# Three loads of x on ScalarE's queue, and the first block of x transposed into a bank of its own

## The chip, the cores and the metric

The kernel runs on one core of one Trainium2 chip. The metric is the device time of one execution in microseconds (us); lower is better. TensorE (PE) multiplies matrices, VectorE (DVE), ScalarE (ACT) and GpSimd (POOL) work element by element, and SyncE (SP) issues transfers between device memory and the core's own memory. A profile shows one execution; times in it count from the start of its span.

## The reference

One decoder block on 256 tokens of width 1024, all in float32. Cut to what matters here:

```python
u = rmsnorm(h, norm_mix_pre[l])          # h is x at first: 256 x 1024
z = u @ w_in[l]                          # 1024 x 4096
p = z[..., :o_q]
q = z[..., o_q:o_k].reshape(B, S, N_HEADS, HEAD_DIM)
k = z[..., o_k:o_v].reshape(B, S, N_HEADS, HEAD_DIM)
v = z[..., o_v:o_g].reshape(B, S, N_HEADS, HEAD_DIM)
g = z[..., o_g:] + b_gate[l]
...                                      # pooling and attention, gated, w_out, residual
u2 = rmsnorm(h, norm_mlp_pre[l])
a = jnp.square(jax.nn.relu(u2 @ w_up[l]))
h = h + rmsnorm(a @ w_down[l], norm_mlp_post[l])
```

The change touches only the start: the loads of x, its transposition, and the products for `v`.

## The kernel before

The 256 tokens are two tiles (t = 0, 1) of 128; the width 1024 is eight blocks (k = 0 to 7) of 128. Every matrix product is made of three: an operand is split into a high part (`_h`, rounded to the multiplier's format) and a low part (`_l`, the rest), and `mm3` adds high by high, high by low and low by high into one accumulator bank. A weight block is loaded raw (`_r`), ACT writes the high part, and DVE (11 of 16 columns) and POOL (the other 5) write the low part (`share_lo`). The order of the work is the order in which the code is written: each engine takes its instructions one by one as they stand, and waits where an operand isn't there.

The kernel starts with the products for `v`. The names:

- `x_sb[t, n]` is one of four pieces of x, 128 tokens by 512 columns (256 KB): n = 0 holds blocks 0 to 3, n = 1 blocks 4 to 7. `load_x(t, n)` issues its load.
- `v_r` with k = 0 to 7 are eight weight pieces, 128 by 512 (256 KB), loaded one by one by `load_v(k)`.
- `turn_x(t, n)` transposes the four blocks of a piece on PE into one bank `x_ps{t}{n}`, which `u_parts(k, t)` reads: ACT scales a block by the gain and writes its high part `uh`, then DVE its low part `ul`. The row factor of the norm is applied later.
- `v_rows(t, k)` is one `mm3` into bank `v_ps{t}`: three products with 512 columns.
- `split_v(k)` makes the high and low part of a weight piece. For k = 0 the high part is made by DVE (a cast), not by ACT.
- `keep_busy(n)` puts n small products of constants on PE.

Eight accumulator banks are in use in turn. All loads at the start are issued by SP, in the order x(0,0), the gain, v0, v1, x(1,0), v2, x(0,1), v3, x(1,1), v4 to v7, then the blocks for q. On PE stand the transposes of x(0,0), nine fillers, the products (t=0, k=0), the transposes of x(1,0), the products (0,1) and (1,0), the transposes of x(0,1), the products (1,1), and so on for k = 2 to 7. After `v` come q, k, p and the gates, pooling and attention, the output projection and the MLP (`up`, `dn`), with weights streamed through three raw buffers.

Of the kernel before, what the change touches and what calls it, by code (L numbers as in the profile page):

```python
# [16 lines left out]
P = 128  # L17
# [3 lines left out]
KD = D // P  # L21
# [12 lines left out]
def hybrid_block(ctx: ExitStack, tc: tile.TileContext, x, norm_mix_pre, w_in, b_gate, pool_w, pool_scale,  # L34
# [4 lines left out]
    nc = tc.nc  # L39
# [10 lines left out]
    def bank(name):  # L50
        return psum.tile([P, 512], F32, tag="bank", name=name)
# [7 lines left out]
    def keep_busy(n):  # L59
        for _ in range(n):  # L60
            nc.tensor.matmul(busy[:, 0:P], fill, fill, start=True, stop=True)
# [6 lines left out]
    ident = const.tile([P, P], F32, name="ident")  # L68
# [81 lines left out]
    def load_next():  # L150
        if done[0] < len(order):
            order[done[0]].load_all()
            done[0] += 1
# [12 lines left out]

    x_sb = act.tile([P, NT, D], F32, name="x_sb")

    def load_x(t, n):
        c = slice(n * 512, (n + 1) * 512)  # L170
        nc.sync.dma_start(x_sb[:, t, c], x[0, t * P:(t + 1) * P, c])


    class Columns:
# [12 lines left out]
        def turn(self):  # L187
            ps = bank(self.name + "_ps")
            nc.tensor.transpose(ps[:, 0:self.n], self.row, ident[0:self.n, 0:self.n])
            nc.vector.tensor_copy(self.col, ps[:, 0:self.n])  # L190
# [4 lines left out]
    g_mix = Columns("g_mix", [(norm_mix_pre, KD)], "oTh")  # L195
# [3 lines left out]
    def load_v(k):  # L199
        bv[k // 4].load(k % 4)  # L200

    load_x(0, 0)
    g_mix.load()
    load_v(0)
    load_v(1)
    load_x(1, 0)
    load_v(2)
    load_x(0, 1)
    load_v(3)
    load_x(1, 1)  # L210
    for k in range(4, KD):
        load_v(k)
    load_next()
    others.load()

# [12 lines left out]
    def mm3(ps, whl, rhl, start, stop, last=0):  # L228

        (wh, wl), (rh, rl) = whl, rhl  # L230
        second, third = ((wh, rl), (wl, rh)) if last == 0 else ((wl, rh), (wh, rl))
        nc.tensor.matmul(ps, wh, rh, start=start, stop=False, skip_group_check=True)  # L232
        nc.tensor.matmul(ps, *second, start=False, stop=False, skip_group_check=True)  # L233
        nc.tensor.matmul(ps, *third, start=False, stop=stop, skip_group_check=True)  # L234
# [23 lines left out]
    def tokens(hl, k, t):  # L258
        c = slice(t * P, (t + 1) * P)
        return hl[0][:, k, c], hl[1][:, k, c]  # L260
# [5 lines left out]
    def narrow(blocks, k, c=slice(0, 512)):  # L266
        b = blocks[k // 4]
        return b.hi[:, k % 4, c], b.lo[:, k % 4, c]

    def placed(pool, blocks, tag, name, at, room=128):  # L270


        t = pool.tile([P, blocks * S + room], F32R, tag=tag, name=name)
        return t[:, at:at + blocks * S].rearrange("p (k s) -> p k s", k=blocks)
# [50 lines left out]
    def scaled_parts(hl, k, t, ps, gain):  # L325
        c = slice(t * P, (t + 1) * P)
        v = ps[:, (k % 4) * P:(k % 4 + 1) * P]
        hi, lo = hl[0][:, k, c], hl[1][:, k, c]
        nc.scalar.activation(hi, v, AF.Copy, scale=gain)
        nc.vector.scalar_tensor_tensor(lo, v, gain, hi.bitcast(F32), op0=ALU.mult, op1=ALU.subtract)  # L330
# [14 lines left out]
    u = tuple(placed(act, KD, f"uT_{i}", f"u{i}", 112) for i in "hl")  # L345
# [6 lines left out]
        yield from rstd(ss, rr[t])  # L352

    def u_parts(k, t):
        scaled_parts(u, k, t, xT[t, k // 4], g_mix[k])

    vps = [bank(f"v_ps{t}") for t in range(NT)]

    def v_rows(t, k, last=0):
        mm3(vps[t], tokens(u, k, t), narrow(bv, k), k == 0, k == KD - 1, last)  # L360
# [3 lines left out]
    xT = {}  # L364

    def turn_x(t, n):
        xT[t, n] = turn(x_sb[:, t, :], n, f"x_ps{t}{n}")

    def split_v(k):
        bv[k // 4].split_piece(k % 4, True)  # L370

    g_mix.turn()
    turn_x(0, 0)
    keep_busy(9)
    nc.vector.tensor_copy(bv[0].hi[:, 0, :], bv[0].raw[:, 0, :])
    u_parts(0, 0)
    bv[0].share_lo(0)
    v_rows(0, 0, last=1)
    u_parts(1, 0)
    turn_x(1, 0)  # L380
    split_v(1)
    v_rows(0, 1)
    u_parts(0, 1)
    v_rows(1, 0)
    turn_x(0, 1)
# [590 lines left out]
```

## Time and profile before

| | us |
|---|---|
| median of 3 runs | 340.37 (340.05 to 341.89) |
| the profiled execution | 339.66 |
| its span (first to last instruction) | 337.9 |
| PE busy | 329.9 (98%) |
| PE's weight loads busy | 305.0 (90%) |
| DVE, ACT, POOL busy | 220.3, 182.2, 77.9 |
| read from device memory | 61.10 MB, 184 GB/s over the span |

Busy time of PE is modelled and overlaps with its weight loads, so 98% says that PE is nearly always in use, not that it runs at its peak. The chain of waits follows the work that ended last back to the start, and names at each step what released it. In lists of waits each row has the time in total, the number of waits and the longest; in timelines each row has the start, the length, the engine, the line, the operation and, in brackets, how long the engine was idle before it and what ended that. SPq and ACTq are the queues in which an engine's transfers are issued; an issue is short, and the transfer lands later.

### The profile page before, as it was taken

How to read it: one execution, taken by the hardware profiler on the slowest of the kernel's cores; microseconds unless marked ns; L12 is line 12 of the kernel's file. 1: busy time of each engine (PE TensorE's matmuls, PEld its weight loads, DVE VectorE, ACT ScalarE, POOL GpSimd, SP SyncE). 2: the span in 40 equal slices, each digit the busy share in tenths (PEclk: the TensorE clock that was granted, in tenths of full speed). 3: DMA queues.
4: the chain of work that ended last, by engine and by line, in shares of the span. 5: the costliest groups of instructions: out<-in, count | busy, mean ns of one | idle time of the engine just before them, and what ended most of it. 6: DMA issues, size and time to landing. Idle time of an engine off the chain costs nothing.

```text
span 337.9 us, 5701 instructions
## 1 busy us (share of the span) xinstructions
PE 329.9 (98%) x2325; PEld 305.0 (90%) x2325; DVE 220.3 (65%) x292; ACT 182.2 (54%) x256; POOL 77.9 (23%) x68
## 2 busy tenths in 40 slices
PE   8999999999999999999999999999999999999992
PEld 7799999999999999888898998989989989899881
DVE  3899777998385789376686746637366374653535
ACT  3984678665837755175768436354263551544331
POOL 3698589155305000056600000000000000000000
PEclk9999999999999999999999999999999999999999
DMA  6996971644555946707355854907629267090003
GB/s 211 375 324 216 222 232 27 237 151 140 209 189 207 353 135 240 248 4 248 124 176 198 288 211 139 330 30 263 236 74 317 109 236 262 11 353 14 0 0 124
DMA packets 27363, 63.04 MB, mean 187 GB/s; under 512 B 1317, under 2 KB 2761, under 8 KB 27337
## 3 DMA queue, kind: packets, MB, share of 16 engines
q1 hardware_dynamic: 26760, 62.15, 53.4%
q0 software_dynamic: 576, 0.52, 1.2%
q8 instruction: 18, 0.29, 0.4%
q14 instruction: 9, 0.07, 0.1%
HBM read 61.10 MB, written 1.05 MB: 184 GB/s over the span
## 4 chain that ended last, share of the span: by engine, by line
PE 96%; DMA 1%; DVE 1%; SPq 0%; DVEq 0%; ACT 0%; issue 0%; ACTq 0%
PE up_ps L232 9%; PE up_ps L234 9%; PE up_ps L233 9%; PE d_ps L242 7%; PE d_ps L241 7%; PE d_ps L245 7%; PE g_ps L232 4%; PE g_ps L233 4%; PE g_ps L234 4%; PE wo_ps L241 2%; PE wo_ps L242 2%; PE wo_ps L245 2%; DMA x_sb<-in_x_dram 1%; PE q_ps L232 1%; PE p_ps L234 1%; PE q_ps L234 1%
## 5 line engine op out<-in xcount | busy, mean ns | idle before, releaser
L232 PE MATMUL up_ps<-u2h,up_h 128*128 128x256 f32 x224 | 62.1, 277 | 0.0
L233 PE MATMUL up_ps<-u2l,up_h 128*128 128x256 f32 x224 | 61.9, 276 | 0.0
L234 PE MATMUL up_ps<-u2h,up_l 128*128 128x256 f32 x224 | 61.9, 276 | 0.0
L93 DVE TENSOR_TENSOR dn_l<-dn_r,dn_h 128x2048 fp32r<-128x2048 f32 x16 | 36.5, 2292 | 16.4 <-ACT dn_h L89 16.3
L233 PEld LDWEIGHTS up_ps<-u2l,up_h 128*128 128x128 f32 x224 | 42.1, 188 | 0.0
L232 PEld LDWEIGHTS up_ps<-u2h,up_h 128*128 128x128 f32 x224 | 42.1, 188 | 0.0
L241 PE MATMUL d_ps<-dn_h,ah 128*128 128x512 f32 x108 | 42.1, 389 | 0.0
L242 PE MATMUL d_ps<-dn_l,ah 128*128 128x512 f32 x108 | 42.1, 389 | 0.0
L234 PEld LDWEIGHTS up_ps<-u2h,up_l 128*128 128x128 f32 x224 | 42.1, 188 | 0.0
L89 ACT ACTIVATE dn_h<-dn_r 128x2048 fp32r<-128x2048 f32 x16 | 30.4, 1915 | 21.2 <-issue 12.8
L892 POOL TENSOR_TENSOR o_out<-o_out,g_mlp_post 128x256 f32<-128x256 f32 x1 | 0.7, 737 | 159.1 <-ACT o_out L891 159.1
L232 PE MATMUL g_ps<-uh,g_h 128*128 128x256 f32 x128 | 35.6, 278 | 0.0
L93 DVE TENSOR_TENSOR up_l<-up_r,up_h 128x2048 fp32r<-128x2048 f32 (+1 forms) x14 | 30.2, 2193 | 8.1 <-ACT up_h L89 8.1
L233 PE MATMUL g_ps<-ul,g_h 128*128 128x256 f32 x128 | 35.3, 276 | 0.0
L234 PE MATMUL g_ps<-uh,g_l 128*128 128x256 f32 x128 | 35.3, 276 | 0.0
L245 PE MATMUL d_ps<-dn_h,al 128*128 128x512 f32 x108 | 33.2, 389 | 0.0
L805 ACT ACTIVATE relu<-up_ps 128x512 f32<-128x512 f32 x16 | 9.5, 597 | 39.4 <-PE up_ps L234 39.4
L89 ACT ACTIVATE up_h<-up_r 128x2048 fp32r<-128x2048 f32 x16 | 29.9, 1904 | 1.6 <-PE wo_ps L245 1.6
L807 DVE TENSOR_TENSOR a<-up_ps,relu 128x512 f32<-128x512 f32 x16 | 11.0, 690 | 28.9 <-ACT relu L805 28.8
L93 POOL TENSOR_TENSOR up_l<-up_r,up_h 128x640 fp32r<-128x640 f32 (+1 forms) x4 | 15.6, 3914 | 44.2 <-ACT up_h L89 44.2
L245 PEld LDWEIGHTS d_ps<-dn_h,al 128*128 128x128 f32 x108 | 20.3, 188 | 4.2
L233 PEld LDWEIGHTS g_ps<-ul,g_h 128*128 128x128 f32 x128 | 24.0, 188 | 0.0
(240 smaller groups left out, 858.0 us busy)
## 6 DMA issues: line engine op xcount, KB each, us to landing
up_r<-in_w_up_dram SPq DMA_DIRECT2D x16, 1024.0 KB, 5.6
dn_r<-in_w_down_dram SPq DMA_DIRECT2D x16, 1024.0 KB, 4.9
g_r<-in_w_in_dram SPq DMA_DIRECT2D x8, 1024.0 KB, 5.5
o_r<-in_w_out_dram SPq DMA_DIRECT2D x4, 1024.0 KB, 5.0
v_r<-in_w_in_dram SPq DMA_DIRECT2D x8, 256.0 KB, 5.4
q_r<-in_w_in_dram SPq DMA_DIRECT2D x4, 512.0 KB, 6.3
k_r<-in_w_in_dram SPq DMA_DIRECT2D x2, 1024.0 KB, 5.9
p_r<-in_w_in_dram SPq DMA_DIRECT2D x2, 1024.0 KB
```

Source lines behind the costliest of these rows:

```text
L89: nc.scalar.activation(self.hi[:, s, :], self.raw[:, s, :], AF.Copy)
L93: eng.tensor_tensor(self.lo[:, s, c], self.raw[:, s, c], self.hi[:, s, c].bitcast(F32), ALU.subtract)
L232: nc.tensor.matmul(ps, wh, rh, start=start, stop=False, skip_group_check=True)
L233: nc.tensor.matmul(ps, *second, start=False, stop=False, skip_group_check=True)
L234: nc.tensor.matmul(ps, *third, start=False, stop=stop, skip_group_check=True)
L241: nc.tensor.matmul(ps, xh, wh[:, c], start=start, stop=False, skip_group_check=True)
L242: nc.tensor.matmul(ps, xh, wl[:, c], start=False, stop=False, skip_group_check=True)
L245: nc.tensor.matmul(ps, xl, wh[:, c], start=False, stop=stop, skip_group_check=True)
L805: nc.scalar.activation(r, ps, AF.Relu)
L807: nc.vector.tensor_tensor(a, ps, r, ALU.mult)
L892: nc.gpsimd.tensor_tensor(o[:, 768:D], o[:, 768:D], g_mlp_post[:, 768:D], ALU.mult)
```

## The change

Three of the four loads of x are issued by ACT, in program order behind its warm-up activation, and SP issues x(0,0), the gain and then v0 to v7 in a row. Block 0 of x(0,0) is transposed into a bank of its own (`first`), and the other three blocks into `x_ps00`. The high and low part of that first block stand ahead of the other transposes in the code, so on DVE ahead of the cast of v0. The fillers go from nine to five. The transposes of x(1,0) stand behind the products (0,1).

```diff
-    def load_x(t, n):
+    def load_x(t, n, queue):
         c = slice(n * 512, (n + 1) * 512)
-        nc.sync.dma_start(x_sb[:, t, c], x[0, t * P:(t + 1) * P, c])
+        queue.dma_start(x_sb[:, t, c], x[0, t * P:(t + 1) * P, c])
...
-    load_x(0, 0)
+    load_x(0, 0, nc.sync)
     g_mix.load()
-    load_v(0)
-    load_v(1)
-    load_x(1, 0)
-    load_v(2)
-    load_x(0, 1)
-    load_v(3)
-    load_x(1, 1)
-    for k in range(4, KD):
+    for k in range(KD):
         load_v(k)
+    for t, n in ((1, 0), (0, 1), (1, 1)):
+        load_x(t, n, nc.scalar)
...
-        scaled_parts(u, k, t, xT[t, k // 4], g_mix[k])
+        scaled_parts(u, k, t, first if (k, t) == (0, 0) else xT[t, k // 4], g_mix[k])
...
     g_mix.turn()
-    turn_x(0, 0)
-    keep_busy(9)
-    nc.vector.tensor_copy(bv[0].hi[:, 0, :], bv[0].raw[:, 0, :])
+    first = bank("x_ps")
+    nc.tensor.transpose(first[:, 0:P], x_sb[:, 0, 0:P], ident)
     u_parts(0, 0)
+    xT[0, 0] = bank("x_ps00")
+    for j in range(1, 4):
+        nc.tensor.transpose(xT[0, 0][:, j * P:(j + 1) * P], x_sb[:, 0, j * P:(j + 1) * P], ident)
+    keep_busy(5)
+    nc.vector.tensor_copy(bv[0].hi[:, 0, :], bv[0].raw[:, 0, :])
     bv[0].share_lo(0)
     v_rows(0, 0, last=1)
     u_parts(1, 0)
-    turn_x(1, 0)
     split_v(1)
     v_rows(0, 1)
+    turn_x(1, 0)
     u_parts(0, 1)
```

PE before, from the products (0,0) on; `v_ps0` and `v_ps1` are the banks of the two token tiles, `x_ps10` and `x_ps01` those of the transposed pieces x(1,0) and x(0,1), and the brackets name the engines or transfers waited for:

```order
L234 MATMUL v_ps0_155<-v_0_l_158,uh_151 128x512 [waits DVE_49,Pool_49]
L322 MATMUL x_ps10_188<-ident_110,x_sb_115 128x128 [waits DMAHW4_49]
L322 MATMUL x_ps10_188<-ident_110,x_sb_115 128x128 x3
L232 MATMUL v_ps0_155<-v_0_h_157,uh_151 128x512 [waits Activation_49]
L233 MATMUL v_ps0_155<-v_0_l_158,uh_151 128x512 [waits DVE_49,Pool_49]
L234 MATMUL v_ps0_155<-v_0_h_157,ul_152 128x512
L232 MATMUL v_ps1_156<-v_0_h_157,uh_151 128x512 [waits Activation_49]
L233 MATMUL v_ps1_156<-v_0_l_158,uh_151 128x512
L234 MATMUL v_ps1_156<-v_0_h_157,ul_152 128x512 [waits DVE_49]
```

The same place on PE now:

```order
L229 MATMUL v_ps0_155<-v_0_l_158,uh_151 128x512 [waits DVE_49,Pool_49]
L227 MATMUL v_ps0_155<-v_0_h_157,uh_151 128x512 [waits Activation_49]
L228 MATMUL v_ps0_155<-v_0_l_158,uh_151 128x512 [waits DVE_49,Pool_49]
L229 MATMUL v_ps0_155<-v_0_h_157,ul_152 128x512
L317 MATMUL x_ps10_191<-ident_110,x_sb_115 128x128 [waits DMAHW3_49]
L317 MATMUL x_ps10_191<-ident_110,x_sb_115 128x128 x3
L227 MATMUL v_ps1_156<-v_0_h_157,uh_151 128x512 [waits Activation_49]
L228 MATMUL v_ps1_156<-v_0_l_158,uh_151 128x512
L229 MATMUL v_ps1_156<-v_0_h_157,ul_152 128x512 [waits DVE_49]
```

The transposes into `x_ps10` moved behind the three products that follow them, so the first product into `v_ps1` stands right behind those transposes.

SP's issues at the start before:

```order
L171 DMA x_sb<-in_x_dram 128x512
L184 DMA g_mix_row<-in_norm_mix_pre_dram 8x128
L80 DMA v_r<-in_w_in_dram 128x512 x2
L171 DMA x_sb<-in_x_dram 128x512
L80 DMA v_r<-in_w_in_dram 128x512
L171 DMA x_sb<-in_x_dram 128x512
L80 DMA v_r<-in_w_in_dram 128x512
L171 DMA x_sb<-in_x_dram 128x512 [waits DMAHW0_49]
L80 DMA v_r<-in_w_in_dram 128x512 [waits DMAHW1_49]
```

SP's issues now:

```order
L171 DMA x_sb<-in_x_dram 128x512
L184 DMA g_mix_row<-in_norm_mix_pre_dram 8x128
L80 DMA v_r<-in_w_in_dram 128x512 x3
L80 DMA v_r<-in_w_in_dram 128x512 [waits DMAHW0_49]
L80 DMA v_r<-in_w_in_dram 128x512 [waits DMAHW1_49]
L80 DMA v_r<-in_w_in_dram 128x512 [waits DMAHW2_49]
```

The three later pieces of x are gone from SP's queue, and every piece of v from the third on moved up.

ACT at the start before, up to its part of v1:

```order
L67 ACT_TABLE_LOAD
L67 ACTIVATE warm_108<-eps_106 128x1 [waits DVE_49]
L329 ACTIVATE uh_151<-x_ps00_164,g_mix_col_117 128x128 [waits DVE_49,PE_49]
L329 ACTIVATE uh_151<-x_ps00_164,g_mix_col_117 128x128 [waits DVE_49]
L89 ACTIVATE v_0_h_157<-v_0_r_122 128x512 [waits DMAHW3_49]
```

ACT at the start now, with the three issues behind its table load and its warm-up:

```order
L67 ACT_TABLE_LOAD
L67 ACTIVATE warm_108<-eps_106 128x1 [waits DVE_49]
L171 DMA x_sb_115<-in_x_dram 128x512 x3
L324 ACTIVATE uh_151<-x_ps_164,g_mix_col_117 128x128 [waits DVE_49,PE_49]
L324 ACTIVATE uh_151<-x_ps00_168,g_mix_col_117 128x128 [waits PE_49]
L89 ACTIVATE v_0_h_157<-v_0_r_122 128x512 [waits DMAHW4_49]
```

The three issues are new, and the second `uh` now reads another bank than the first and waits for PE instead of DVE.

DVE at the same place before:

```order
L190 COPY g_mix_col_117<-g_mix_ps_161 128x8 [waits PE_49]
L375 CAST v_0_h_157<-v_0_r_122 128x512 [waits DMAHW2_49]
L330 SCALAR_TENSOR_TENSOR ul_152<-x_ps00_164,g_mix_col_117,uh_151 128x128 [waits Activation_49]
L93 TENSOR_TENSOR v_0_l_158<-v_0_r_122,v_0_h_157 128x352 [waits DVE_49]
L330 SCALAR_TENSOR_TENSOR ul_152<-x_ps00_164,g_mix_col_117,uh_151 128x128 [waits Activation_49]
L93 TENSOR_TENSOR v_0_l_158<-v_0_r_122,v_0_h_157 128x352 [waits DMAHW3_49,Activation_49]
```

DVE there now:

```order
L190 COPY g_mix_col_117<-g_mix_ps_161 128x8 [waits PE_49]
L325 SCALAR_TENSOR_TENSOR ul_152<-x_ps_164,g_mix_col_117,uh_151 128x128 [waits Activation_49]
L376 CAST v_0_h_157<-v_0_r_122 128x512 [waits DMAHW2_49]
L93 TENSOR_TENSOR v_0_l_158<-v_0_r_122,v_0_h_157 128x352 [waits DVE_49]
L325 SCALAR_TENSOR_TENSOR ul_152<-x_ps00_168,g_mix_col_117,uh_151 128x128 [waits Activation_49]
L93 TENSOR_TENSOR v_0_l_158<-v_0_r_122,v_0_h_157 128x352 [waits DMAHW4_49,Activation_49]
```

The cast of v0 moved behind the first `ul`.

More of the change, by code (lines that the diff above doesn't have):

```diff
@@ L372, in hybrid_block @@
     g_mix.turn()
-    turn_x(0, 0)
-    keep_busy(9)
+    first = bank("x_ps")
+    nc.tensor.transpose(first[:, 0:P], x_sb[:, 0, 0:P], ident)
+    u_parts(0, 0)
+    xT[0, 0] = bank("x_ps00")
+    for j in range(1, 4):
+        nc.tensor.transpose(xT[0, 0][:, j * P:(j + 1) * P], x_sb[:, 0, j * P:(j + 1) * P], ident)
+    keep_busy(5)
     nc.vector.tensor_copy(bv[0].hi[:, 0, :], bv[0].raw[:, 0, :])
-    u_parts(0, 0)
     bv[0].share_lo(0)
```

## The prediction

> **What bounds the kernel now.** I read the page's first lines and chain of waits, then what the TensorE (PE) waits for over the whole run.
>
> ```profile
> span 337.9 us, 5701 instructions
> PE 329.9 (98%) x2325; PEld 305.0 (90%) x2325; DVE 220.3 (65%) x292; ACT 182.2 (54%) x256; POOL 77.9 (23%) x68
> PE 96%; DMA 1%; DVE 1%; SPq 0%; DVEq 0%; ACT 0%; issue 0%; ACTq 0%
> ...
> PE busy L61 <- PEq L962: 0.8, 1, 0.8
> PE x_ps L322 <- DMA x_sb<-in_x_dram: 0.3, 1, 0.3
> PE v_ps L234 <- DVE v_l L93: 0.2, 1, 0.2
> ```
>
> PE is 96% of the chain, and its only waits for operands in 337.9 us add up to 0.5 us (counted between the modelled ends of its instructions). So whatever moves the start of PE's unbroken stretch moves the end one for one. The chain in order of time shows where that stretch begins; the timeline of PE shows what lies around it.
>
> ```profile
> 1.99 0.43 SPq L80
> ...
> 2.46 4.58 DMA x_sb<-in_x_dram
> ...
> 7.09 0.66 PE x_ps L322 x4
> ...
> 3.63 1.11 PE L322 MATMUL x_ps<-ident,x_sb 128*128 128x128 f32 x4
> 4.54 0.98 PE L61 MATMUL busy<-const-bfloat16-1.0 128*128 128x128 bf16 x9
> 6.33 0.47 PE L234 MATMUL v_ps<-v_l,uh 128*128 128x512 f32 x1 [0.24 <-DVE v_l L93]
> 7.82 0.40 PE L233 MATMUL v_ps<-v_l,uh 128*128 128x512 f32 x1
> 8.06 0.39 PE L234 MATMUL v_ps<-v_h,ul 128*128 128x512 f32 x1
> 8.29 0.42 PE L232 MATMUL v_ps<-v_h,uh 128*128 128x512 f32 x1
> ```
>
> Write x10 for the first half of the second token tile, v0 and v1 for the first two weight pieces, P(t,k) for the three products of tile t with piece k. P(0,0) ends about 6.6 (6.33 and a pitch of 0.24); PE then waits until x10, issued at 2.46, lands at 7.04. Its transposes run at 7.09, P(0,1) fills the time in which ScalarE (ACT) makes the operand of P(1,0), and P(1,0) follows at 8.29, right behind 8.06. From there PE does not stop. The yardstick is therefore when P(1,0) starts: all that PE has done by then is the same in both kernels.
>
> **The new order on PE.** P(0,1) now stands ahead of the transposes of x10. So P(0,1) can use the wait before 7.04, but P(1,0) comes a full round trip behind the transposes (7.09 to 8.29, 1.20 us) with nothing on PE to cover it: what follows P(1,0) in the order is the next transposes. And the transposes now wait for P(0,1), which needs v1 split. The rows of that split:
>
> ```profile
> 4.78 0.37 ACT L329 ACTIVATE uh<-x_ps,g_mix_col 128x128 fp32r<-128x128 f32 x1 [2.55 <-PE x_ps L322]
> 5.57 0.37 ACT L329 ACTIVATE uh<-x_ps,g_mix_col 128x128 fp32r<-128x128 f32 x1 [0.42 <-DVE ul L330]
> 5.83 0.62 ACT L89 ACTIVATE v_h<-v_r 128x512 fp32r<-128x512 f32 x1
> ...
> 4.77 0.43 DVE L375 CAST v_h<-v_r 128x512 fp32r<-128x512 f32 x1 [0.86 <-DMA v_r<-in_w_in_dram]
> 5.18 0.35 DVE L330 SCALAR_TENSOR_TENSOR ul<-x_ps,g_mix_col,uh 128x128 fp32r<-128x128 f32 x1
> 5.45 0.74 DVE L93 TENSOR_TENSOR v_l<-v_r,v_h 128x352 fp32r<-128x352 f32 x1
> ...
> 5.28 0.53 POOL L93 TENSOR_TENSOR v_l<-v_r,v_h 128x160 fp32r<-128x160 f32 x1 [2.85 <-DVE v_h L375]
> 6.53 0.86 POOL L93 TENSOR_TENSOR v_l<-v_r,v_h 128x160 fp32r<-128x160 f32 x1 [0.72 <-ACT v_h L89]
> ...
> DMA to landing us min/median/max: 3.5/3.5/3.5
> ```
>
> The last row is v1 alone: issued at 1.99, landed at 5.49. With that landing unchanged: the second u operand of the first tile moves up from 5.57 to 4.78 (it no longer waits for VectorE, DVE, to leave a shared bank), so ACT is free at 5.15 and v_h(1) runs 5.53 to 6.15; POOL starts its part of v_l(1) 0.08 later (as 6.53 follows 5.83+0.62) and takes 0.86, to 7.09; PE takes the second product of P(0,1) 0.14 later (as 6.33 follows 5.45+0.74), 7.23, the third at 7.47, the transposes at 7.71, and P(1,0) 1.20 later, 8.91. Against 8.29 that is **+0.6 us**, although x10 is long there. Earlier landings hardly mend it. Had v0 and v1 landed at once, DVE's cast of v0, now behind the first ul, would start at 4.91 (first transpose from 3.63, 0.47 for the longest of the four, by the row below; then 0.04 to ACT, 0.37, 0.04 and 0.35), POOL's two parts would run 5.42 to 5.95 and 5.95 to 6.81, and P(1,0) would start at 8.63, +0.3; with POOL's second part as short as its first (0.53) and no lag beyond 0.05, 8.2, a tenth earlier. So this term lies between -0.1 and +0.6; I take +0.6, since nothing ahead of v1 on SP's queue is removed.
>
> ```profile
> L322 PE MATMUL x_ps<-ident,x_sb x16: 270/272/474, 3.6 to 12.1; 128*128 128x128 f32 x16
> ```
>
> **The bank of its own.** The first u operand starts at 4.14 instead of 4.78. P(0,0) gains at most 0.1 (cast at 4.91 to 5.34 instead of 4.77 to 5.20 takes it back), and that lies inside the wait for v_l(1): nothing. The bank holds one block, no instruction is added, the four transposes are the same. Four fewer fillers are some 0.4 us of PE (nine in 0.98) taken out of a stretch in which PE waits for v_l(0) anyway: nothing.
>
> **The queue.** Three issues of 0.43 us leave SP's queue and go to ACT's, behind its table load and the warm-up activation:
>
> ```profile
> 0.74 1.28 ACT L67 ACT_TABLE_LOAD   x1 [0.74 <-PEq L962]
> 2.03 0.20 ACT L67 ACTIVATE warm<-eps 128x1 f32<-128x1 f32 x1
> ...
> 1.60 0.82 SPq L80 DMA_DIRECT2D v_r<-in_w_in_dram  x2
> 2.46 0.43 SPq L171 DMA_DIRECT2D x_sb<-in_x_dram  x1
> ...
> 0.00:1.50 1.50, 0.72 (x8) 0.75 (x9) 0.06 (x1) 0.76 (x1) 0.89 (x7) 1.00 0.00 0
> 1.50:3.10 1.60, 1.60 (x18) 1.60 (x17) 0.00 (x0) 0.72 (x2) 0.93 (x4) 1.00 0.69 218
> 2.50:10.00 7.50, 6.97 (x44) 5.35 (x42) 3.58 (x10) 3.05 (x9) 1.85 (x3) 1.00 0.86 273
> 10.00:17.50 7.50, 7.50 (x36) 5.98 (x35) 6.52 (x19) 7.03 (x17) 5.41 (x7) 1.00 1.05 389
> ```
>
> (last three columns of the windows: granted clock, DMA share, GB/s). ACT's three issues end by 3.5, before its first work at 4.14, so ACT itself loses nothing. SP issues v2 and later pieces up to 2 us sooner, into a queue of DMA engines that is already full: no gain for v0 and v1, which were ahead of x10 on SP all along. What does change is that x10 no longer stands behind v1. The first x piece, issued at 0.74, moved no byte before 1.5, a lag of 0.8; x10, issued behind the warm-up at 2.23, is thus ready at 3.1. By then 218 GB/s x 1.6 us = 349 KB have moved, the first x piece (262 KB) and a third of v0. A piece takes 262 KB / 273 GB/s = 0.96 us. The remaining two thirds of v0 and the whole of v1 share the engines with x10 and x01. If both queues get half, v1 is late by 1.67 x 0.96 = **1.6 us**.
>
> The trace has one place with two queues at work, POOL's copies beside SP's load:
>
> ```profile
> 35.00:36.50 1.50, 1.50 (x16) 1.50 (x15) 0.84 (x2) 1.17 (x2) 0.63 (x2) 1.00 1.16 325
> ...
> q1 hardware_dynamic: 183, 0.37, 86.1%
> q0 software_dynamic: 125, 0.11, 29.8%
> ```
>
> The second queue took 125 of 308 packets (41%) and 23% of the bytes, its packets being 1 KB; the sum (325 GB/s) did not grow. At 23% v1 would be late by 1.6 x 0.23/0.77 = 0.5, at 41% by 1.1, at half by 1.6. I take half, since x's packets are as large as v's and the packet share is near it. [...]
>
> v1's lateness goes in full into P(0,1), the transposes behind it and P(1,0). The later pieces have room: the share of DVE and POOL for k from 2 on follows P(1,0)'s chain, and v2 to v7 come earlier on SP. The q pieces wait for the landings of x01 and v2 before SP issues them (lanes reused), which costs nothing while PE itself is late.
>
> **The sum.** +0.6 (order) +1.6 (v1) = +2.2 us. The profiled execution took 339.66 us (span 337.9 and 1.8 around it), 0.7 below the median of 340.37; the sum gives 341.9 for it and 342.6 for the median.
>
> **Rivals.**
>
> - *Less than half for ACT's queue*: v1 late by 0.5 to 1.1, the sum +1.1 to +1.7: 341.5 to 342.1. For it, the byte share at 35 us; against it, that queue's packets were half as large.
> - *ACT issues early*: the three issues start at 0.74, beside the table load, not behind it. Then the whole of x10, x01 and x11 may lie beside the first x piece, v0 and v1: v1 late by up to 3 x 0.96 = 2.9, the sum +3.5, 343.9. Against it, POOL's first copy, which began only when POOL's work ahead of it ended though its input had been there since 29.1:
>
> ```profile
> 27.55 4.64 POOL L447 TENSOR_SCALAR prob<-dist 128x384 f32<-128x384 f32 x2
> 32.26 0.82 POOL L485 DMA_DIRECT2D stacked<-stacked  x1
> L484 ACT ACTIVATE stacked<-q_ps x4: 586/594/595, 28.5 to 35.3; 64x512 fp32r<-64x512 f32 x4
> ```
>
>   [...]
> - *Order of issue kept*: v1 lands as before; +0.6, 341.0. Against it, the row at 35 us.
> - *Not slower*: the DMA engines were busy for 0.86 of 2.5 to 10 us and 1.05 later, so ACT's queue could fill idle time, x10 land well ahead, and v0 and v1 come sooner too. It needs v1 by about 4.7 and POOL at 0.53 for its second part; then P(1,0) starts at 8.2 to 8.3 and the time is 340.3 to 340.4. Against it, v1 would have to take 0.8 less than now with three more transfers beside it.
>
> **How the numbers follow.** Half share 0.38, less than half 0.20, early issue 0.22, order kept 0.12, not slower 0.08. Half a per cent, 1.7 us, is about what a measurement of this kernel can tell from no change. Above +1.7 lie most of the half share (0.32 of 0.38, its share being uncertain by some 0.3 us), nearly all of early issue (0.21) and a quarter of less than half (0.05): 0.58 slower. Faster by 0.5% would need P(1,0) at 6.6, ahead of any chain above: 0.02. The rest, 0.40, is within. The likeliest case alone spans 342.1 to 343.2; the range, 340.5 to 344.2, leaves out part of the last case below and an early issue with more above.
>
> **What would show it.** In the changed kernel's trace: the issue time of ACT's three DMAs (2.2 or 0.8); v1's landing (7.1 by the half share, 5.5 to 6.6 otherwise) with x10's well ahead of it; PE idle in front of the second product of P(0,1), put down to v_l, POOL or ACT, where it used to wait for x_sb; and a second idle stretch of some 0.5 us between the transposes of x10 and P(1,0). From there on PE unbroken, and every later stage shifted by one amount. Wrong would be: v1 landing before 5.3; or a granted clock below 1.00 after the longer wait (it was 1.00 in all windows above), which would add up to 6 x 0.23 = 1.4 us for the six products near it.

## The result, and the profile after

The changed kernel takes 344.65 us (median of 343.58, 345.67, 343.85 and 345.46), against 340.21 for the kernel before on the same chip: a ratio of 1.0136, 95% interval 1.0111 to 1.0160. It is slower by 4.4 us; 2.2 were predicted, and 344.65 lies above the range. The profiled execution took 343.58, the lowest of the four, with a span of 341.8. One execution of e1 (682.79 us, the profiled one) and one of e12 (428.19 us) ran slow from end to end and are left out of the medians below.

What PE waits for, from the view of waits of the changed kernel (us in total, times, longest):

```profile
PE v_ps L227 <- DVE v_h L376: 1.9, 1, 1.9
PE g_mix_ps L189 <- DMA g_mix_row<-in_norm_mix_pre_dram: 1.1, 1, 1.1
PE busy L61 <- PEq L962: 0.8, 1, 0.8
PE v_ps L227 <- ACT uh L324: 0.5, 1, 0.5
```

The wait for x_sb is gone. In its place stand three: for the gain, for v0 (its cast, on DVE), and the round trip from the transposes of x10 to P(1,0). The timelines of ACT and its queue, and of PE, show where they lie:

```profile
0.74 1.28 ACT L67 ACT_TABLE_LOAD   x1 [0.74 <-PEq L962]
0.91 1.34 ACTq L171 DMA_DIRECT2D x_sb<-in_x_dram  x3
...
4.56 0.24 PE L189 MATMUL g_mix_ps<-ident,g_mix_row 8*128 8x8 f32 x1 [1.06 <-DMA g_mix_row<-in_norm_mix_pre_dram]
...
8.30 0.77 PE L227 MATMUL v_ps<-v_h,uh 128*128 128x512 f32 x1 [1.92 <-DVE v_h L376]
8.86 0.63 PE L228 MATMUL v_ps<-v_h,ul 128*128 128x512 f32 x1
9.29 0.66 PE L229 MATMUL v_ps<-v_l,uh 128*128 128x512 f32 x1
...
11.12 1.05 PE L317 MATMUL x_ps<-ident,x_sb 128*128 128x128 f32 x4
12.63 0.51 PE L227 MATMUL v_ps<-v_h,uh 128*128 128x512 f32 x1 [0.46 <-ACT uh L324]
12.98 0.39 PE L228 MATMUL v_ps<-v_l,uh 128*128 128x512 f32 x1
```

Three things are to be seen. ACT's queue issues at 0.91, while the table load (0.74 to 2.02) still runs and ahead of the warm-up (2.04). P(1,0), the prediction's yardstick, starts at 12.63 in place of 8.29, 4.34 later. And PE is slow until then: the products of P(0,0) follow each other by 0.43 to 0.56 us (8.30, 8.86, 9.29), where those of P(0,1) followed by 0.24 to 0.32 before; the four transposes take 1.05 in place of 0.66.

The view of landings gives v0 (issued at 1.60), then v1 (issued at 2.0), then x10 (issued at 0.91):

```profile
DMA to landing us min/median/max: 6.1/6.1/6.1
DMA to landing us min/median/max: 6.5/6.5/6.5
DMA to landing us min/median/max: 4.2/4.2/4.2
```

So x10 lands near 5.1 and v0 and v1 at 7.70 and 8.45, against 4.75 and 5.48 before: both about 3 us later. The DMA view shows why, by queue (q1 is SP's, q10 ACT's; packets, MB, share of the engines), first for 2.5 to 4.5 us and then for 4.5 to 7.0:

```profile
q10 hardware_dynamic: 210, 0.40, 67.7%
q1 hardware_dynamic: 65, 0.08, 15.8%
...
q1 hardware_dynamic: 241, 0.45, 58.8%
q10 hardware_dynamic: 211, 0.37, 39.9%
```

In the first stretch ACT's queue has 210 of 275 packets: x10 and x01, issued at 0.91 and 1.33, are under way, v0 hardly is. In the second the two queues share by packets, 241 to 211. The total does not grow in the first stretch (0.48 MB; before, SP alone moved 0.49); in the second it is 0.82 MB against 0.68, a fifth more. By 8.0 all of ACT's 432 packets had moved, so the whole of x10, x01 and x11 went ahead of the end of v1 (8.45).

Behind P(1,0) the prediction's "every later stage shifted by one amount" holds nearly: tile by tile, PE is 4.44 later at q and k, and 3.93 later from 44 us to the end. The 0.5 is made up at the scores (40 to 44 us); several of the kernels below do it too, and what decides it is not shown.

### The profile page after: what moved, and what is told of

Same layout as the page of the kernel before. It is cut to its first block, busy times and chain, and to the rows that moved or that the text cites. A ratio compares the mean times of both kernels' runs of the same rounds, so it can differ in the third digit from the quotient of the medians.

```text
span 341.8 us, 5693 instructions
## 1 busy us (share of the span) xinstructions
PE 330.9 (97%) x2321; PEld 305.5 (89%) x2321; DVE 219.2 (64%) x292; ACT 182.2 (53%) x256; POOL 78.6 (23%) x68
## 3 DMA queue, kind: packets, MB, share of 16 engines
HBM read 61.10 MB, written 1.05 MB: 182 GB/s over the span
## 4 chain that ended last, share of the span: by engine, by line
PE 95%; DMA 2%; DVE 1%; ACT 0%; SPq 0%; issue 0%; DVEq 0%; ACTq 0%
PE up_ps L227 9%; PE up_ps L229 9%; PE up_ps L228 9%; PE d_ps L237 7%; PE d_ps L236 7%; PE d_ps L240 7%; PE g_ps L227 4%; PE g_ps L228 4%; PE g_ps L229 4%; PE wo_ps L236 2%; PE wo_ps L237 2%; PE wo_ps L240 2%; DMA v_r<-in_w_in_dram 2%; PE v_ps L227 1%; PE v_ps L228 1%; PE v_ps L229 1%
```

## The experiments

Times are medians, each beside runs of the kernel before on its chip (340.26 for e1 to e4, 339.97 for e5 to e8, 340.0 for e9 to e12). "Full clock" is when the trace's clock records first grant PE its full clock, in the profiled execution; it is 5.17 in the kernel before and 12.57 in the changed one.

| kernel | us | ratio, 95% interval | full clock | P(1,0) |
|---|---|---|---|---|
| changed | 344.65 | 1.0136 (1.0111 to 1.0160) | 12.57 | 12.63 |
| e1 queue only | 343.3 | 1.0083 (1.0053 to 1.0114) | - | - |
| e2 order only | 341.21 | 1.0027 (1.0004 to 1.0049) | 3.68 | 9.22 |
| e3 changed, more fillers | 343.2 | 1.0093 (1.0059 to 1.0126) | 9.51 | 12.47 |
| e4 ACT's issue at 4.1 | 346.05 | 1.0157 (1.0124 to 1.0190) | 5.42, lost 8.84 to 15.66 | 11.32 |
| e5 ACT's issue at 2.1 | 345.34 | 1.0161 (1.0145 to 1.0178) | 4.08, lost 7.49 to 14.32 | 10.75 |
| e6 before, few opening fillers | 340.05 | 1.0007 (0.9990 to 1.0024) | 7.85 | 8.60 |
| e7 changed, all gaps filled | 342.7 | 1.0079 (1.0064 to 1.0095) | 4.08 | 11.66 |
| e8 gain alone on ACT | 339.9 | 0.9995 (0.9985 to 1.0005) | 3.99 | 8.50 |
| e9 ACT's issue at 2.3, filled | 341.81 | 1.0044 (1.0026 to 1.0062) | 6.73 | 10.48 |
| e10 queue only, filled | 342.02 | 1.0066 (1.0043 to 1.0090) | 5.82 | 11.29 |
| e11 v0 and v1 on ACT | 340.3 | 1.0005 (0.9994 to 1.0016) | 9.61 | 10.14 |
| e12 v0 on ACT | 340.47 | 1.0017 (1.0005 to 1.0029) | 9.53 | 10.10 |

### The two halves of the change: e1 and e2

e1 is the kernel before with the three x loads on ACT; e2 is the changed kernel with all loads on SP in the old order.

> The kernel before with one edit: x(1,0), x(0,1), x(1,1) issued by ACT, SP issues x(0,0), the gain, v0 to v7. PE's order, the bank and the nine fillers stay as before. Theory A (the queue costs most): ACT issues at 0.9, ahead of v0 and v1, and the transfers are served about in order of issue, so v0 and v1 land near 7.7 and 8.5 as in the changed kernel; PE can transpose x(1,0) early and the products (1,0) follow (0,1) without a gap, so 343.3 to 344.2, that is +3 to +4. Theory O (the order on PE costs most): v0 and v1 late, but hidden, 340.2 to 341.5.

> The changed kernel with all loads back on SP in the order of before; the bank, the five fillers and the new order on PE stay. Theory A: v1 lands at 5.5 again and only the new order is left, the +0.6 of the prediction: 340.8, between 340.3 and 341.2, with the first product of (1,0) at 8.8 to 8.9. Theory O: most of the 4.4 us stays, 342 or more.

The queue alone costs 3.0 us, as theory A had it, and the order alone 0.95, at the upper edge of what was expected; together that is 4.0 of the 4.4 (e10 below shows the landings with the queue alone). In e2 the waits of PE name the new round trip:

```profile
PE v_ps L232 <- DVE v_h L381: 1.2, 1, 1.2
PE busy L61 <- PEq L967: 0.8, 1, 0.8
PE v_ps L232 <- ACT uh L329: 0.5, 1, 0.5
```

P(1,0) starts 0.93 later there; 0.45 of that is v1, which in this execution landed at 5.93 without any change to its queue ahead of it. So the order by itself is near the +0.6 of the prediction or under it.

### The issue held back: e4, e5 and e9

In these, ACT's three issues stand behind an activation that waits for DVE's memsets, so that they come at a chosen time. e4 has five memsets, as cut here, e5 two; `t2` and `late` are new tiles.

```diff
-    for k in range(KD):
...
+    for _ in range(5):
+        nc.vector.memset(t2, 1.0)
+    load_v(0)
+    load_v(1)
+    nc.scalar.activation(late, t2[:, 0:1], AF.Copy)
+    load_x(1, 0, nc.scalar)
+    load_v(2)
...
```

> The changed kernel with ACT's three issues held back to about 2.2 us, behind an activation that waits for five DVE memsets of a scratch tile, so behind SP's issues of v0 and v1. Order-of-issue theory: v0 and v1 land at 4.8 and 5.5 as before, x(1,0) near 7, and only the order on PE is left, 340.6 to 341.4. Half-share theory of the prediction: v1 lands near 7.1 beside x(1,0), 342.2 to 342.8 and more if the clock is late too. If a semaphore wait does not hold back ACT's issues, they stand at 0.9 again and the time is that of the changed kernel.

> The changed kernel with ACT's three x issues held by an activation that waits for two VectorE memsets (480 ns each, the second ends near 2.1), so that x10 is issued near 2.25, between SP's issues of v1 (2.0) and v2 (2.45), as the prediction had assumed. Served in order of issue (theory): v0 lands near 4.8, v1 near 5.5 to 5.7, x10 near 7, and the time is that of the new order alone, 340.8 to 341.4. Half share between the two queues (the prediction's own term, the rival): v1 lands near 7.1 and the time is near 342.6.

Both missed, by 2.7 us at the least. The hold itself worked, as the timeline of ACT in e4 shows:

```profile
4.10 0.20 ACT L210 ACTIVATE late<-t 128x1 f32<-128x1 f32 x1 [1.87 <-DVE g_mix_col L190]
4.11 1.34 ACTq L171 DMA_DIRECT2D x_sb<-in_x_dram  x3
```

Here the issue stands behind an activation that waits for a semaphore, and it came with it (4.11 and 4.10); in the changed kernel it stands behind the table load and came at 0.91, 1.11 before that load ended (2.02). The warm-up of the changed kernel waits for DVE as well, but DVE's memset ended at 0.87, so 0.91 fits the same reading. In e4, with the issue at 4.11, v0 and v1 landed at 4.91 and 5.64, about as before, and x10 at 9.70. In e5, with the issue at 2.13, v0 landed at 5.00 and v1 at 6.58, together with x10 (6.74): neither order of issue (v1 5.5) nor quite the half share as I had sized it (7.1).

Two costs hid these results. The first is PE's clock. The windows of e5 (length, busy time of each engine, granted clock, DMA share, GB/s):

```profile
0.67:4.08 3.41, 3.30 (x27) 3.11 (x28) 1.20 (x4) 1.58 (x3) 1.61 (x6) 1.00 0.55 160
4.08:7.49 3.41, 2.10 (x13) 1.17 (x11) 1.80 (x5) 1.36 (x3) 1.05 (x2) 1.00 0.95 320
7.49:10.91 3.42, 2.66 (x8) 1.53 (x7) 0.47 (x2) 0.37 (x1) 0.68 (x1) 0.50 1.04 392
10.91:14.32 3.41, 3.41 (x10) 2.74 (x11) 2.81 (x9) 3.20 (x9) 1.90 (x3) 0.50 0.96 338
```

(PE's busy time is the first number behind the length.) PE had its full clock from 4.08, was busy for only 2.10 of the next 3.41 us, and lost half the clock for the 6.83 us after that. The second cost lies far from the change: between 85 and 134 us both kernels lose another 1.7 us, evenly, which the changed kernel does not. Both hold an added tile (`t2`, `late`); e9 has none.

So e9 puts the memsets into the part of x_sb that is loaded last, and 14 fillers in place of 5 behind the first transposes.

> As the kernel with the issue held to 2.1 (v1 there landed at 6.6, together with x10, 1.1 later than before), but the memsets go into the part of x that lands last, so that no tile is added, and 14 in place of 5 fillers stand behind the first transposes. Theory: half share sets v1 at 6.5 to 6.7, P(1,0) starts 1.0 to 1.4 later than before, the full clock once granted stays, the even slow-down between 85 and 134 us of the two kernels with an added tile is gone: 341.0 to 341.7. Rival: what those two lost late belongs to ACT's later issue itself: 343 or more.

The timelines of ACT and PE in e9:

```profile
2.26 0.20 ACT L208 ACTIVATE warm<-x_sb 128x1 f32<-128x1 f32 x1
2.27 1.35 ACTq L171 DMA_DIRECT2D x_sb<-in_x_dram  x3
...
10.48 0.50 PE L235 MATMUL v_ps<-v_h,uh 128*128 128x512 f32 x1 [0.46 <-ACT uh L332]
```

and v1 (issued at 2.0) in the view of landings:

```profile
DMA to landing us min/median/max: 5.2/5.2/5.2
```

Here ACT's issue comes at 2.27, where the prediction had put it (2.23). v1 lands at 7.21 (7.1 predicted), P(1,0) starts at 10.48 (8.29 + 2.2 = 10.49 predicted), and the time is +1.8 us (+2.2 predicted; interval 0.9 to 2.1, so a little less). The loss between 85 and 134 us is gone, so it did not come from the later issue. The queues between 4.5 and 7.0:

```profile
q10 hardware_dynamic: 187, 0.35, 43.4%
q1 hardware_dynamic: 169, 0.30, 33.1%
```

ACT's queue took 187 of 356 packets, half. Much of the agreement is luck. ACT's first packets moved at 4.3, 2.0 us after the issue, not 0.8 as the prediction took from SP's first load. And the trace counts a landing in 16 parts: 15 of v1's had come by 6.22, 0.7 later than all of v1 before, and the last came at 7.21. In e5, with the issue at nearly the same time, v1 was 1.1 late. The fair partner of e9 is e7 below, the same order with fillers and the early issue: 342.7, 0.9 more, with P(1,0) 1.18 later.

### PE's clock: e3, e6 and e7

e3 and e7 are the changed kernel with more fillers (e3: 27 in place of 5 behind the first transposes; e7: 40 there, and 38 in place of 24 at the start). e6 is the kernel before with 2 in place of 24 at the start.

> The changed kernel with 27 fillers in place of five, so that PE is busy in its wait for v0. Theory C (part of the loss is TensorE's clock, granted at 12.6 instead of 5.2 because PE stood idle): granted near 5 to 7, six products at a pitch of 0.23 instead of 0.43 (1.2 us) and four transposes 0.3 faster, so 1.2 to 1.8 less than the changed kernel, 342.9 to 343.4. Without C: the products start as late and run as fast, 344.4 to 345 (fillers that outlast the wait would add to it).

> The changed kernel with 38 opening fillers in place of 24 and 40 in place of 5 behind the first transposes, so that PE has work from 1.7 until v0 is cast. Theory (landings set +3, the rest of +4.4 is the clock): full clock near 5.2 in place of 12.57, products of P(0,0) and P(0,1) at a pitch of 0.24 in place of 0.43, transposes of x10 0.66 in place of 1.05, P(1,0) near 11.3 in place of 12.63: 342.8 to 343.4. Rival (landings and order set all of it): 344.6. If v0's landing alone counted (+3.0), 343.2 as well, but with P(1,0) at 11.3.

e3 takes 343.2, as expected, but not by the way expected: the full clock came only at 9.51 and P(1,0) at 12.47. Its fillers stand behind the first transposes and so leave open the 1.1 us that PE waits for the gain ahead of them, and v0 and v1 landed at 8.05 and 9.20 in that execution, 0.35 and 0.75 later than in the changed kernel.

e7 takes 342.7 (342.62 to 342.9): the same loads, the same order, 1.95 us less than the changed kernel by the medians and 0.57% by the two ratios, a tenth below what was expected. v0 still lands at 7.5. PE's timeline in e7:

```profile
8.13 0.47 PE L227 MATMUL v_ps<-v_h,uh 128*128 128x512 f32 x1 [0.34 <-DVE v_h L376]
8.45 0.39 PE L228 MATMUL v_ps<-v_h,ul 128*128 128x512 f32 x1
...
10.60 0.60 PE L317 MATMUL x_ps<-ident,x_sb 128*128 128x128 f32 x4
11.66 0.51 PE L227 MATMUL v_ps<-v_h,uh 128*128 128x512 f32 x1 [0.46 <-ACT uh L324]
```

The first two products now follow by 0.32, the transposes take 0.60, and P(1,0) starts 0.97 earlier than in the changed kernel; 0.84 of that lies behind the second product of P(0,1) (10.04 to 11.66 in place of 10.17 to 12.63), the rest is v1, which landed a little earlier. So the fillers are worth 1.95 us between the medians, and 2.7 of the 4.4 are left for the landings and the order; the traces show 0.84 of it as the clock. The changed kernel was profiled in the fastest of its four executions, so how the slower ones lose more is not shown. The windows of the changed kernel, in steps of 3.41 us (the time for which e5 had its full clock) back from its own first full clock (12.57), show how busy PE was ahead of it; below them stand those of the kernel before, up to its first full clock (5.17) and behind it:

```profile
2.33:5.74 3.41, 2.35 (x17) 2.02 (x16) 0.27 (x2) 0.37 (x1) 0.10 (x1) 1.00 0.89 262
5.74:9.16 3.42, 1.50 (x8) 0.88 (x7) 1.49 (x5) 1.00 (x2) 0.86 (x1) 1.00 1.02 386
9.16:12.57 3.41, 3.02 (x9) 1.87 (x8) 0.50 (x1) 0.36 (x1) 0.86 (x1) 1.00 0.91 316
```

```profile
1.76:5.17 3.41, 3.41 (x28) 3.13 (x26) 0.57 (x2) 0.83 (x3) 0.67 (x3) 1.00 0.85 264
5.17:8.58 3.41, 2.88 (x18) 1.88 (x15) 2.15 (x6) 1.26 (x4) 1.39 (x2) 1.00 0.82 267
```

(In these two views the clock column reads 1.00 ahead of the first record too; the products show the half clock: in the changed kernel the last two of P(0,1) follow by 0.42 and 0.52 ahead of 12.57, those of P(1,0) by 0.35 and 0.23 behind it.) PE's busy time of 2.35 and 1.50 of 3.41 brought no full clock, 3.02 and 3.41 did. The waits for the gain and for v0 lie in the two windows without.

> The kernel before with 2 in place of 24 opening filler products on PE; loads, order and data are as before. Theory (the late full clock is a cost of its own): PE's first work is then at 3.43 in place of 1.69, the full clock comes at 7 to 9 in place of 5.17, the transposes of x10 take 1.05 in place of 0.66 and the products of P(0,1) run at a pitch of 0.43 in place of 0.24, so P(1,0) starts 0.9 later and what follows runs at half pace until the clock is granted: 341.2 to 342.5, with landings unchanged. Rival (the clock costs nothing, only landings do): 340.3.

A miss that limits the theory: without opening fillers the full clock came at 7.85, 2.7 later than before, the products of P(0,0) followed by 0.42 to 0.57, the transposes took 1.04 in place of 0.66, and the time did not change (340.05 against 339.97). In the kernel before PE waits 0.3 us for x10 in that stretch; in e6 the transposes start no later (7.02, before 7.09), and P(1,0) started only 0.3 later, as PE's timeline in e6 shows:

```profile
7.02 1.04 PE L322 MATMUL x_ps<-ident,x_sb 128*128 128x128 f32 x4
7.79 0.50 PE L232 MATMUL v_ps<-v_h,uh 128*128 128x512 f32 x1
...
8.60 0.42 PE L232 MATMUL v_ps<-v_h,uh 128*128 128x512 f32 x1
```

So a clock 2.7 us later cost nothing measurable here, while between the changed kernel and e7, from the second product of P(0,1) on, the half clock cost 0.84 on the way to P(1,0).

### The queue without the clock: e10

> The queue alone (order and bank of before, the three x issues on ACT at 0.91) with 38 and 40 fillers in place of 24 and 9, so that PE's clock comes early. Theory: x10 5.1, v0 7.5, v1 8.4 as in the changed kernel; P(1,0) follows P(0,1) without a round trip, near 10.8 in place of 11.66 with the new order: 341.7 to 342.2, that is 0.6 to 0.9 less than the changed kernel with fillers (342.7). Rival (the order costs nothing once the landings are late): 342.7.

342.02, within what was expected, and 0.7 under e7, the same loads with the new order (0.4 by the two ratios). The two intervals overlap, but the sign is that of e2. It is also 1.3 under e1, the same kernel without the added fillers (0.6 by the two ratios). P(1,0) starts at 11.29 rather than the 10.8 expected, because v0 and v1 landed at 8.08 and 8.91 in this execution, some 0.5 later than in e7; PE waits for v0's cast there:

```profile
8.68 0.47 PE L227 MATMUL v_ps<-v_h,uh 128*128 128x512 f32 x1 [0.23 <-DVE v_h L370]
```

### Looking for a faster version: e8, e11 and e12

> The kernel before, with one edit: the small load of g_mix (4 KB) goes over ACT's queue, issued near 0.91, and all x and v pieces stay on SP in their order, each 0.43 earlier. Served in order of issue: x00 as before, v0 near 4.4, v1 near 5.1, x10 near 6.7 in place of 7.04; P(1,0) up to 0.4 earlier: 339.8 to 340.1. Rival (the transfers are bound by the engines, not by the issue): within 0.2 of 340.3.

> The kernel before with v0 and v1 over ACT's queue (issued 0.91 and 1.36) and x00, g_mix, x10 and the rest over SP's (x10 issued at 1.60 in place of 2.46), and 30 opening fillers in place of 24. Theory (two queues start more transfers early and share): x00 near 4.0, v0 near 5.2, v1 and x10 by 6.4 in place of 5.5 and 7.04, P(1,0) up to 0.6 earlier: 339.4 to 339.9. Rival (sharing delays x00 and v0 as much as it brings x10 forward): 340.0 to 340.8.

> As the kernel before, with v0 alone over ACT's queue (issued 0.91), v1 on SP at 1.60, x10 at 2.02, and 30 opening fillers. Theory: x00 up to 0.5 later, v0 near 4.5, v1 near 5.5, x10 near 6.5: 339.5 to 340.0. Rival (bytes, not issues, set x10's landing): 340.0 to 340.5.

None is faster. e8 moves every large issue on SP behind the first 0.4 earlier and gains nothing that can be measured: P(1,0) starts at 8.50, with x10, issued at 2.10, landed only at 7.3. That 339.9 lies in the range expected is luck, since P(1,0) came later and not earlier. In e11 and e12 the gain's 4 KB load suffers as in the changed kernel, behind two large transfers (x(0,0), issued at 0.74, and one issued by ACT at 0.91; the gain at 1.17 to 1.18). PE waits for it for 0.87 in e11 and 0.86 in e12, 1.06 in the changed kernel; in e11:

```profile
5.01 0.24 PE L189 MATMUL g_mix_ps<-ident,g_mix_row 8*128 8x8 f32 x1 [0.87 <-DMA g_mix_row<-in_norm_mix_pre_dram]
```

The first transposes move from 3.43 to 5.01 (the six fillers added end at 4.14, then PE waits for the gain), the clock comes at 9.5 to 9.6, and what x10 gains (landed at 6.3 in e11, 7.0 in e12, 7.04 before) is given back: its transposes run at 8.4, behind P(0,0). Both were profiled in an execution near the slow end of theirs (340.9 each), so these traces show more loss than the medians do.

## Why the prediction was wrong

- **The failed step is the issue time.** The prediction put ACT's issues "behind its table load and the warm-up activation", at 2.23; the trace has 0.91. It leaned on POOL's queue, whose first copy came at 32.26, behind POOL's work up to 32.19; ACT's first issue came at 0.91, beside a table load from 0.74 to 2.02. The rival *ACT issues early* (0.22) was the one that came true, and its price was right: v1 late by 2.9 (measured 2.97), P(1,0) by 3.5 (measured 3.37 in e7, with the clock taken out). Between e9 and e7, one with the issue at 2.27 and one at 0.91, P(1,0) moves by 1.18 and the median by 0.9; the prediction's two cases are 1.3 apart.
- **The second miss is a term that was left out of the sum.** The prediction named the clock only as what would make it wrong, at up to 1.4 us, and it read the clock column's 1.00 as a full clock from the start, where the first record came at 5.17 (the four transposes at 3.63 took 1.11, those at 7.09 took 0.66). The runs show 0.84 in the two profiled executions and 1.95 between the medians of e7 and the changed kernel. That a longer wait would come was part of the forecast, so the clock belonged in the sum and in the range.
- **Half share held by packets** where both queues had work: 241 to 211 in the changed kernel, 187 to 169 in e9. The term made from it, +1.6, came out at 1.1 in e5 and 1.73 in e9, the latter by one late part of v1, so e9's agreement with the sum (P(1,0) at 10.48, +1.8 us) does not prove how the term comes about. *Order of issue kept* looked right at first, since x10 and x01 landed ahead of v0 (5.15 and 6.88 against 7.70); but in e5 and e9 v1, issued before x10 (2.0 against 2.13 and 2.27), came 1.1 and 1.73 later than before.
- **+0.6 for the order** was about right: +0.95 in e2 with v1 0.45 late, 0.7 between the medians of e10 and e7.
- **v0 and the gain were overlooked.** The sum delayed v1 alone. With the issue at 0.91 the first x piece (4.15 in place of 3.35), the gain (4.42 in place of 3.10) and v0 are all late, and the first wait of PE for an operand is for the gain.
- **The bank of its own** gave nothing, as said: PE waits 1.9 us for v0 behind it.
- *Not slower* asked for v1 by 4.7; it came at 8.45.

## What to carry to other kernels

Before moving a load to another queue, find when that queue will really issue (here at 0.91, not at 2.23), and list everything that is then in front of the transfers that the start waits for, the smallest included (the 4 KB of the gain landed at 4.42 in place of 3.10): here a second queue took 210 of 275 packets and then 211 of 452 while the start waited for the first one's transfers, and the total grew by a fifth at most (0.82 MB in place of 0.68). To hold an issue back, an activation that waits for a semaphore served here (issue at 4.11 in e4, the activation at 4.10); a table load placed ahead of it did not (issue at 0.91, end of the load at 2.02). Where a change lets PE idle for one or two microseconds at a time (1.06 and 1.92 here), price its clock as well (1.95 us between the medians of the changed kernel and e7), and test by filling the gap with products of constants before blaming the data.

## What was not expected of the hardware

- PE's clock changed in steps of 3.41 us: in e5 it was granted from 4.08 to 7.49 and then withheld to 14.32 (3.41 and 6.83), in e4 granted from 5.42 to 8.84 and withheld to 15.66 (3.42 and 6.82), and in the kernel before it was granted for 331.09 us, in the changed one for 327.68, one step less. The phase differed from one execution to the next: counted back in such steps, the first full clock leads to 1.76 in the kernel before (from 5.17), 2.33 in the changed one (from 12.57) and 0.67 in e5 (from 4.08). Full clock came at the end of a step with 2.88 us (e2), 3.02 (changed), 3.30 (e5 and e7) and 3.41 (before) of modelled PE work, and not after 2.35 and 1.50 (changed) or 2.66 (e5); it was lost after steps with 1.86 (e4) and 2.10 (e5, so 1.3 us of idleness in 3.4), and kept after one with 2.03 (e2), so this busy time alone does not tell when it is lost. The phase would explain why the changed kernel's four times fall into two groups, 343.6 to 343.9 and 345.5 to 345.7, while e7's lie within 0.3 us; but landings vary as well (v1 at 8.39 to 9.20 in the changed kernel, e3, e7 and e10), and only one of the four was profiled, so neither is shown.
- With ACT's issue at 0.91 a few parts of the first x piece came late: 14 of its 16 by 3.19 in the changed kernel, the last two at 4.00 and 4.15, and likewise at 4.16 to 4.26 in e3, e7 and e10. With SP alone the last came at 3.35, 0.13 behind the one ahead of it. In the changed kernel the first transpose stood at 4.73, behind the wait for the gain, which landed at 4.42.
- The first packets of ACT's queue moved 1.6 to 2.4 us after their issue (issued at 0.91, moved at 2.5 in the changed kernel; 4.11 and 6.5 in e4), SP's first after 1.0 (0.74 and 1.75).
- e4 and e5 lost 1.75 us between 85 and 134 us against the kernel before (3.6%), with the clock fully granted. An added tile is what they share and the others lack; that it is the cause, and why, is not shown.
